# Logits in three rounded products, one key block among the first chunks, and a last half in two quarters

## The chip, the cores and the metric

The kernel runs on one core of a Trainium2 chip. The metric is the device time of one execution in microseconds (us). The engines are TensorE (PE; its weight loads are PEld), VectorE (DVE), ScalarE (ACT), GpSimd (POOL) and SyncE (SP, which only issues transfers here).

## The reference

A trunk of two layers on 512 tokens of 1024 values. Layer A mixes by gated linear attention (six heads) and attention into 256 memory tokens; layer B by stick-breaking attention (twelve heads of 64) and memory attention. After each mixer come an output projection, a residual and a layer norm, and then PEER, a feed-forward layer of retrieved experts, with its own residual and layer norm.

```python
def gla_layer_mixer(x, mem, w_in, w_gate2, b_gate, head_g, w_mem_kv, w_out):
    proj = x @ w_in
    q, k, v, r, glr, qm = jnp.split(proj, A_IN_SPLITS, axis=-1)
    log_g = jax.nn.log_sigmoid((glr @ w_gate2 + b_gate).astype(jnp.float32)) / GLA_TAU
...
def stick_breaking(q, k, v):
    B, H, T, d = q.shape
    scale = d ** -0.5
    outs = []
    for i in range(T // SB_BLOCK):
        t0, t1 = i * SB_BLOCK, (i + 1) * SB_BLOCK
        z = jnp.einsum('bhtd,bhsd->bhts', q[:, :, t0:t1], k[:, :, :t1]).astype(jnp.float32) * scale
...
        log_A = jax.nn.log_sigmoid(z) + lax.cumsum(log_not, axis=3, reverse=True) - log_not
        A = jnp.where(mask, jnp.exp(log_A), 0.0).astype(v.dtype)
        outs.append(jnp.einsum('bhts,bhsd->bhtd', A, v[:, :, :t1]))
...
        h = layer_norm(DEEPNORM_ALPHA * h + mix, ln_g[layer, 0], ln_b[layer, 0])
        ffn = peer(h, peer_w_q[layer], peer_subkeys[layer], peer_u[layer], peer_v[layer])
        h = layer_norm(DEEPNORM_ALPHA * h + ffn, ln_g[layer, 1], ln_b[layer, 1])
```

## The kernel before, in words

Nearly all products are made of three: an operand is split into a rounded high part (fp32r, by ACT) and the rounded rest (by DVE), and high x high, high x low and low x high add up in PSUM. `stat_mm` does this for one block of 128 output rows over the eight chunks of the 1024 inner values, lines L117 to L119 for each chunk, 512 tokens at a time. `split` (L97 on ACT, L98 on DVE) makes the two parts. Several stretches are under a manual schedule: there the engines named run in the order in which the code is written.

*Start of mixer A.* `values_gates` multiplies all eight chunks of x (its transpose, loaded by `load_xT`, split at L470 and L471) with 272 weight columns (256 of values, 16 of gates; `load_vg`, split at L479 and L480), for four tiles of 128 tokens, three matmuls each (L498 to L500, tile `vga`). SP issues the loads in the order of the calls, and ACT and DVE do the splits in that order too. Then `stat_units` goes through eight blocks (`as` is the load, `ash` and `asl` its halves, `asp` the result in PSUM): blocks 0 to 2 the keys, 3 to 5 the queries, 6 and 7 the memory queries. `ev_stat` copies each to SBUF with ACT. Between them `gate_logits` puts its transposes (`pgl`, L513) and the later gate work.

*Mixer B.* The twelve heads go in six pairs. For a pair, one `bsp` block holds the keys and one the queries, 64 rows for each head; `ev_stat` (L744) copies them to SBUF as `kq`, queries times 0.125. `logits` (L764, tile `pz`) multiplies them by blocks of 128 queries against all keys up to that block: query block 3 (512 columns), blocks 2 and 0 (384 and 128), and block 1 (256), in plain fp32. The first head has array rows 0 to 63, the second 64 to 127, each with its own PSUM buffer. DVE clips at L767 (`zs`), ACT takes exponent and logarithm (L771, L777), DVE scans and subtracts (L782, L783), ACT exponentiates (L787). `turn` transposes the weights of an earlier pair (`pt`, L796) and copies them out with DVE (L800) or ACT (L802); `attend` multiplies them with the values (`pav`, L810). One period of the loop (j = 1 to 5) makes the logits of pair j, the weights of pair j - 1 turned, and the next pair's blocks; the last makes the values instead (`bva`). PE, DVE and ACT run in the written order there.

*End.* The last tile of the last PEER takes its six tail matrices for the first half of 512 columns, then for the second half (L1789 to L1791, `acc`, 18 matmuls each). `layer_norm` then makes y = alpha x + acc (L993), the statistics (L995), their aggregate (L998) and the scaled result (L1002 to L1010), which goes out by DMA (L1675).

Of the kernel before, what the change touches and what calls it, by code (L numbers as in the profile page):

```python
# [10 lines left out]
F32 = mybir.dt.float32  # L11
# [63 lines left out]
def psum(E, name="ps", tag="ps"):  # L75
    p, tags = E.ps
    return p.tile([P, 512], F32, tag=tag, name=name, bufs=tags[tag])
# [48 lines left out]
def stat_units(E, src, blks, evac, xhi=None, xlo=None, n=T, name="sp", tag="ps"):  # L126

    for b in blks:
        hi, lo = split(E, load_raw(E, src[b], name), name)
        ps = psum(E, name=f"{name}p", tag=tag)  # L130
        stat_mm(E, ps[:, :n], hi, lo, xhi, xlo)
        evac(b, ps[:, :n])
        yield
# [279 lines left out]
def mixer_a(E, a):  # L413
# [4 lines left out]
    with tc.tile_pool(name="acat", bufs=1, reuse_waits="tile") as ap:  # L418
# [11 lines left out]
        with psum_pool(E, acc=4, ps=4), tc.tile_pool(name="mixwk", bufs=2, reuse_waits="tile") as wk, \  # L430
# [52 lines left out]
            def values_gates():  # L483

                acc = [psum(E, name="vga", tag="acc") for _ in range(NT)]
                ws = load_vg(0, 1)
                load_xT(0, 1)
                load_xT(1, 1)
                ws += load_vg(1, 2)
                load_xT(2, 2)  # L490
                load_xT(4, 2)
                ws += load_vg(3, 3)
                load_xT(6, 2)
                ws += load_vg(6, 2)
                for c, h, l in ws:
                    for t in range(NT):
                        xh, xl = E.xhi[:, c, t * P:(t + 1) * P], E.xlo[:, c, t * P:(t + 1) * P]
                        nc.tensor.matmul(acc[t][:, :VG], xh, h, start=(c == 0), stop=False)  # L498
                        nc.tensor.matmul(acc[t][:, :VG], xl, h, start=False, stop=False)
                        nc.tensor.matmul(acc[t][:, :VG], xh, l, start=False, stop=(c == NC - 1))  # L500
                for t in range(NT):
                    twice = gl[:, t, :64].rearrange("p (a b) -> p a b", a=2)[:, :, :16]
                    nc.scalar.activation(twice, acc[t][:, None, 256:VG].to_broadcast([P, 2, 16]), AF.Copy)
                    nc.vector.tensor_sub(gl[:, t, 64:80], acc[t][:, 256:VG], gl[:, t, :16].bitcast(F32))
                for t in range(NT):
                    nc.vector.tensor_copy(v[:, t, 512:], acc[t][:, :256])
# [119 lines left out]

            with tc.manual_schedule(engines={mybir.EngineType.PE}):
                values_gates()
                st = stat_units(E, wst, range(8), ev_stat, name="as")
                logits = gate_logits()  # L630
                for _ in st:
                    next(logits, None)
# [84 lines left out]
def mixer_b(E, wst, wnat, wo, lng, lnb):  # L717

    nc, tc = E.nc, E.tc
    with tc.tile_pool(name="bcat", bufs=1, reuse_waits="tile") as cp:  # L720
# [10 lines left out]
        with tc.tile_pool(name="mbx", bufs=1, reuse_waits="tile") as mp, tc.tile_pool(name="mbwk", bufs=2, reuse_waits="tile") as wk:  # L731
# [3 lines left out]

            kq = {}

            def ev_stat(b, ps):
                if b >= 12:
                    dst = qm[:, b - 12]  # L740
                else:
                    dst = wk.tile([P, T], F32, tag=("kT", "qT")[b % 2], name="kq", bufs=1)
                    kq[b] = dst
                act.append(nc.scalar.activation(dst, ps, AF.Copy, scale=0.125 if b < 12 and b % 2 else 1.0))  # L744

            tiles, act = {}, []

            def logits(g, tags=("z",)):

                two = (g, g + 1)  # L750
                for h in two:
                    zs = wk.tile([P, 1280], F32, tag="zs", name="zs") if g % 4 else new_zs("zs", 1280)
                    tiles[h] = zs, wk.tile([P, 1280], F32, tag="ez", name="ez", bufs=4)
                kT, qT = kq[g], kq[g + 1]
                for n, qs in enumerate(((3,), (2, 0), (1,))):
                    if n:
                        yield
                    pz = [psum(E, name="pz", tag=tags[n % len(tags)]) for _ in two]
                    w, o = sum(i + 1 for i in qs) * P, QO[qs[0]]
                    for i in qs:  # L760
                        c = QO[i] - o
                        for k in range(2):
                            rows = slice(64 * k, 64 * k + 64)
                            nc.tensor.matmul(pz[k][:, c:c + (i + 1) * P], qT[rows, i * P:(i + 1) * P], kT[rows, :(i + 1) * P], start=True, stop=True)  # L764
                    m = (3 - qs[0]) * P
                    for k, h in enumerate(two):
                        nc.vector.tensor_tensor(tiles[h][0][:, o:o + w], pz[k][:, :w], lim[:, m:m + w], op=ALU.min)  # L767
# [90 lines left out]
            with psum_pool(E, ps=2, z=4, c=2), tc.manual_schedule(engines={eng.PE, eng.DVE, eng.Activation}):  # L858
# [11 lines left out]
                def stat(b, ps=None):  # L870

                    ps = ps or psum(E, name="bsp")
                    hi, lo = parts.pop(b)
                    for c in range(NC):
                        stat_mm(E, ps, hi, lo, cs=(c,))
                        yield
                    ev_stat(b, ps)
                    yield

                vacc = []  # L880

                def values(u):

# [24 lines left out]
                for j in range(1, 6):  # L908
# [1 line left out]
                    last = j == 5  # L910
                    zz = logits(h)
                    turn(g, 0, "v")
                    turn(g, 1, "v")
                    next(zz)
                    next(zz)
                    turn(g, 2, "v")
# [14 lines left out]
                    steps(fill)  # L931
                    remain(h)
                    remain(h + 1)
                    weights(h)
                    if not last:
                        fill = stat(h + 3)
# [2 lines left out]
                        prep(*((wst, h + 4) if j < 4 else (wnat, 4)))()  # L939
                        weights(h + 1)  # L940
                        steps(fill)
                        low.append(prep(*((wst, h + 5) if j < 4 else (wnat, 5))))
                    else:
                        late = []
# [36 lines left out]
def layer_norm(E, lp, t, halves, gam, bet, hooks=()):  # L981
# [2 lines left out]
    nc = E.nc  # L984
    y = lp.tile([P, D], F32, tag="lny", name="lny", bufs=1)
    wd = min(h.shape[-1] for h in halves)
    st = E.lnp.tile([P, 2, 6], F32, tag="lnst", name="lnst", bufs=2)
    mv = E.lnp.tile([P, 2], F32, tag="lnmv", name="lnmv", bufs=2)
    sm = E.lnp.tile([P, 4], F32, tag="lnsm", name="lnsm", bufs=2)
    c = 0  # L990
# [67 lines left out]
LEAD = 3  # L1058
TAIL = 6
G3 = 96  # L1060
WOI = 3
RB = 4
SEG = [(0, 1, 0, 16, 16), (1, 1, 16, 8, 8), (2, 1, 24, 8, 5), (3, 1, 32, 8, 4), (4, 1, 40, 4, 3), (5, 3, 44, 4, 2), (8, 8, 56, 1, 1)]
# [2 lines left out]
def peer(E, mixer, wq, sk, ut, vt, un, lng, lnb, out_dram=None, follow=()):  # L1066
# [10 lines left out]
    with ExitStack() as pp:  # L1077
# [659 lines left out]
        with written:  # L1737
# [39 lines left out]
            for t in range(ND):  # L1777
                sl = slice(t * P, (t + 1) * P)
                parts = acc[t]
                if t < ND - 1:  # L1780
                    for k, (whi, wlo, hi, lo) in enumerate(tail):
                        mov_mm(E, parts, whi[:, sl], wlo[:, sl], hi, lo, False, k == TAIL - 1)
                else:
                    c = 0
                    for a in parts:
                        hs = slice(c, c + a.shape[-1])
                        c = hs.stop
                        for k, (whi, wlo, hi, lo) in enumerate(tail):
                            nc.tensor.matmul(a, whi[:, sl], hi[:, hs], start=False, stop=False)  # L1789
                            nc.tensor.matmul(a, whi[:, sl], lo[:, hs], start=False, stop=False)  # L1790
                            nc.tensor.matmul(a, wlo[:, sl], hi[:, hs], start=False, stop=k == TAIL - 1)  # L1791
                if last:
                    finish(t + 1, parts)
                elif t < ND - 1:
                    if t == 0:
                        E.low.pop(0)()
                    finish(t + 1, parts, (lambda: x_to_T(E, t), lambda: E.low.pop(0)()))
                else:
                    finish(t + 1, parts)
# [87 lines left out]
```

## Time and profile before

| | us |
|---|---|
| median of 3 runs | 2839.48 |
| lowest, highest | 2837.48, 2840.02 |
| profiled execution, its own time | 2838.77 |
| its span in the trace | 2837.0 |
| value gates and key block 0 of mixer A | 5.18 to 26.23 |
| one period of mixer B (second of the loop) | 1513.71 to 1532.27 |
| start of the last matmul | 2828.20 |

The span runs from the first to the last record of the trace; the execution's own time has 1.8 us around it. In the rows of the trace stand a start, a length, the engine, the line, the operation, out<-in by the program's names, the shape and, in brackets, the idle time before it with the one that ended it.

### The profile page before, as it was taken

Reading aid. Unit: us, or ns where it says so; the run is one execution under the profiler, and the core shown is the slowest. Engines: PE = TensorE matmul, PEld = TensorE weight load, DVE = VectorE, ACT = ScalarE, POOL = GpSimd, SP = SyncE. Lnnn points to the kernel's source line nnn. Section 1 sums busy time; section 2 is a strip of 40 time slices with the busy share of each in tenths; the row PEclk is TensorE's granted clock in tenths of the full one; section 3 lists DMA queues with packets and bytes.
Section 4 is the critical chain, followed back from the end, with each engine's and each line's share of the span. In section 5 each row is a group of like instructions: output and inputs, shape, how many; then the busy total and the mean of one; then the engine's idle time right before and its main releaser. Section 6 shows DMA issues by size and latency. Waiting matters only on the chain.

```text
span 2837.0 us, 44540 instructions
## 1 busy us (share of the span) xinstructions
PE 2820.4 (99%) x16141; PEld 2509.1 (88%) x16141; DVE 2407.4 (85%) x4917; ACT 1444.6 (51%) x2724; POOL 783.6 (28%) x585
## 2 busy tenths in 40 slices
PE   9999999999999999999999999999999999999998
PEld 8888999999999888888887889999999998888887
DVE  5567999999886888888968879999998878888888
ACT  6342447767774333334446424476677743334333
POOL 0100243333342233245100002433334433333330
PEclk9999999999999999999999999999999999999999
DMA  6332589999999999999721325999999999999994
GB/s 203 101 109 74 179 308 331 334 328 337 352 365 344 341 371 372 366 358 378 238 68 52 112 84 199 317 320 334 335 339 340 379 334 351 372 372 371 370 371 170
DMA packets 311150, 806.99 MB, mean 284 GB/s; under 512 B 32177, under 2 KB 124561, under 8 KB 304529
## 3 DMA queue, kind: packets, MB, share of 16 engines
q1 hardware_dynamic: 195936, 414.93, 42.2%
q0 software_dynamic: 78336, 285.25, 27.7%
q10 hardware_dynamic: 36656, 103.97, 9.5%
q8 instruction: 126, 2.06, 0.3%
q14 instruction: 96, 0.78, 0.1%
HBM read 708.32 MB, written 94.68 MB: 283 GB/s over the span
## 4 chain that ended last, share of the span: by engine, by line
PE 91%; DVE 7%; DMA 1%; issue 1%; ACT 0%; DVEq 0%; ACTq 0%
PE ph L117 11%; PE acc L289 11%; PE acc L291 11%; PE acc L293 11%; PE ph L119 11%; PE ph L118 11%; PE pg L1525 2%; PE pg L1526 1%; DVE ul L98 1%; PE pq L117 1%; PE pq L118 1%; PE pq L119 1%; PE bsp L117 1%; PE bsp L119 1%; PE bsp L118 1%; PE oacc L289 1%
## 5 line engine op out<-in xcount | busy, mean ns | idle before, releaser
L117 PE MATMUL ph<-xhi,uh 128*128 128x368 f32 x2048 | 686.9, 335 | 0.0
L119 PE MATMUL ph<-xhi,ul 128*128 128x368 f32 x2048 | 674.5, 329 | 1.1 <-DVE ul L98 0.8
L118 PE MATMUL ph<-xlo,uh 128*128 128x368 f32 x2048 | 673.5, 329 | 0.0
L1116 POOL DMA_INDIRECT gr<-in_un,gidx x256 | 394.0, 1539 | 802.4 <-DVE gr L1169 588.6
L97 ACT ACTIVATE vh<-vr 128x1024 fp32r<-128x1024 f32 x248 | 262.8, 1060 | 502.2 <-PE acc L293 418.8
L1116 POOL DMA_INDIRECT gr<-in_vt,gidx x256 | 314.2, 1227 | 652.5 <-DVE va L1188 565.4
L289 PE MATMUL acc<-vh,whi 128*128 128x512 f32 x1480 | 455.9, 389 | 0.6 <-ACT whi L1732 0.6
L291 PE MATMUL acc<-vl,whi 128*128 128x512 f32 x1480 | 455.7, 389 | 0.0
L293 PE MATMUL acc<-vh,wlo 128*128 128x512 f32 x1480 | 455.6, 389 | 0.0
L98 DVE TENSOR_TENSOR vl<-vr,vh 128x1024 fp32r<-128x1024 f32 x248 | 303.6, 1224 | 151.1 <-ACT vh L97 150.1
L97 ACT ACTIVATE uh<-ur 128x1024 fp32r<-128x1024 f32 x288 | 304.2, 1056 | 191.9 <-PE ph L118 147.5
L98 DVE TENSOR_TENSOR ul<-ur,uh 128x1024 fp32r<-128x1024 f32 x288 | 351.3, 1220 | 43.6 <-ACT uh L97 42.0
L119 PEld LDWEIGHTS ph<-xhi,ul 128*128 128x128 f32 x2048 | 384.7, 188 | 3.5 <-DVE ul L98 3.5
L118 PEld LDWEIGHTS ph<-xlo,uh 128*128 128x128 f32 x2048 | 385.4, 188 | 0.0
L117 PEld LDWEIGHTS ph<-xhi,uh 128*128 128x128 f32 x2048 | 385.1, 188 | 0.1
L289 PEld LDWEIGHTS acc<-vh,whi 128*128 128x128 f32 x1480 | 277.6, 188 | 58.8 <-ACT whi L1732 1.5
L291 PEld LDWEIGHTS acc<-vl,whi 128*128 128x128 f32 x1480 | 277.7, 188 | 58.0 <-DVE vl L98 0.4
L293 PEld LDWEIGHTS acc<-vh,wlo 128*128 128x128 f32 x1480 | 277.7, 188 | 57.8 <-DVE wlo L1733 0.3
L1169 DVE SCALAR_TENSOR_TENSOR gr<-gr,xnat 128x1024 f32<-128x1024 f32 x256 | 310.0, 1217 | 19.5 <-DMA gr<-in_un,gidx 19.2
L1188 DVE SCALAR_TENSOR_TENSOR va<-gr,gw,va 128x1024 f32<-128x1024 f32 x254 | 325.0, 1280 | 1.3 <-DMA gr<-in_vt,gidx 0.4
L1506 ACT ACTIVATE obl<-ob,rat 128x128 f16<-128x128 f16 x736 | 234.2, 392 | 31.3 <-ACT gt L1529 16.3
L1732 ACT ACTIVATE whi<-w 128x384 fp32r<-128x384 f32 x256 | 131.3, 513 | 96.8 <-DVE w L1721 92.5
(379 smaller groups left out, 4202.5 us busy)
## 6 DMA issues: line engine op xcount, KB each, us to landing
ur<-in_ut SPq DMA_DIRECT2D x256, 512.0 KB
vr<-in_vt SPq DMA_DIRECT2D x256, 512.0 KB
Gd<-gt ACTq DMA_DIRECT2D x48, 1024.0 KB
Ad<-act ACTq DMA_DIRECT2D x112, 368.0 KB
al<-Ad SPq DMA_DIRECT2D x112, 368.0 KB
gl<-Gd SPq DMA_DIRECT2D x26, 1536.0 KB
ur<-in_wq SPq DMA_DIRECT2D x32, 512.0 KB
bs<-in_b_st SPq DMA_DIRECT2D x14, 512.0 KB
```

What stands on the lines that cost most here:

```text
L97: nc.scalar.activation(hi, raw, AF.Copy)
L98: sub = lambda: eng.tensor_sub(lo, raw, hi.bitcast(F32))
L117: nc.tensor.matmul(ps, h, xhi[:, c, sl], start=(c == 0), stop=False)
L118: nc.tensor.matmul(ps, h, xlo[:, c, sl], start=False, stop=False)
L119: nc.tensor.matmul(ps, l, xhi[:, c, sl], start=False, stop=(c == NC - 1))
L289: nc.tensor.matmul(acc[hf], lh, hi[:, hf * 512:(hf + 1) * 512], start=first, stop=False)
L291: nc.tensor.matmul(acc[hf], lh, lo[:, hf * 512:(hf + 1) * 512], start=False, stop=False)
L293: nc.tensor.matmul(acc[hf], ll, hi[:, hf * 512:(hf + 1) * 512], start=False, stop=last)
L1116: nc.gpsimd.indirect_dma_start(out=gr, out_offset=None, in_=tab, in_offset=bass.IndirectOffsetOnAxis(ap=idx[:, k:k + 1], axis=0))
L1169: nc.vector.scalar_tensor_tensor(gr, gr, 1.0, xr, op0=ALU.mult, op1=ALU.mult, accum_out=dst[:, k:k + 1])
L1188: nc.vector.scalar_tensor_tensor(va, gr, gw[:, k:k + 1], va, op0=ALU.mult, op1=ALU.add)
L1506: nc.scalar.activation(obl[:, q], ob[:, q, 0], AF.Copy, scale=rat[:, n0 + q:n0 + q + 1])
```

## The change

Four edits. First, `values_gates` begins with six fp32 matmuls on the identity into an unused PSUM buffer (`idle`), loads key block 0 after the second load of weights, and lets that block's eight chunks follow the value gates one chunk behind; `stat_units` then has blocks 1 to 7. The load of weights 3 to 5 goes ahead of the x chunks 4 and 5. Second, in mixer B keys and queries are kept as a rounded high part (`kqh`, ACT) and a rounded rest (`kql`, a new DVE instruction that reads PSUM), and each logit product is three fp32r matmuls in place of one fp32 matmul, the two heads in turn; in the loop the rests are put off to two places (`rests`). Third, the copy of `turn(g, 1)` goes from DVE to ACT. Fourth, the last half of the last tile is done as two quarters of 256 columns, the first without a stop of its own, and that tile's statistics are taken by 256 columns.

```diff
             def values_gates():
 
                 acc = [psum(E, name="vga", tag="acc") for _ in range(NT)]
+                idle, pa = psum(E, name="idle"), psum(E, name="asp")
+                for _ in range(WARM):
+                    nc.tensor.matmul(idle[:, :P], E.ident, E.ident, start=True, stop=True)
+                place = mp.tile([P, 2, D], F32R, tag="mr", name="as0")
                 ws = load_vg(0, 1)
                 load_xT(0, 1)
                 load_xT(1, 1)
                 ws += load_vg(1, 2)
+                a0 = split(E, load_raw(E, wst[0], "as"), "as", lambda name: place[:, "hl".index(name[-1])])
                 load_xT(2, 2)
+                ws += load_vg(3, 3)
                 load_xT(4, 2)
-                ws += load_vg(3, 3)
                 load_xT(6, 2)
                 ws += load_vg(6, 2)
...
                         nc.tensor.matmul(acc[t][:, :VG], xh, l, start=False, stop=(c == NC - 1))
+                    if c:
+                        stat_mm(E, pa, *a0, cs=(c - 1,))
+                stat_mm(E, pa, *a0, cs=(NC - 1,))
+                ev_stat(0, pa)
...
-                st = stat_units(E, wst, range(8), ev_stat, name="as")
+                st = stat_units(E, wst, range(1, 8), ev_stat, name="as")
...
-            def ev_stat(b, ps):
+            def ev_stat(b, ps, later=None):
                 if b >= 12:
                     dst = qm[:, b - 12]
                 else:
-                    dst = wk.tile([P, T], F32, tag=("kT", "qT")[b % 2], name="kq", bufs=1)
-                    kq[b] = dst
-                act.append(nc.scalar.activation(dst, ps, AF.Copy, scale=0.125 if b < 12 and b % 2 else 1.0))
+                    tag, scale = (("kT", 1.0), ("qT", 0.125))[b % 2]
+                    dst = wk.tile([P, T], F32R, tag=tag, name="kqh", bufs=1)
+                    low = wk.tile([P, T], F32R, tag=tag + "l", name="kql", bufs=1)
+                    kq[b] = dst, low
+                    act.append(nc.scalar.activation(dst, ps, AF.Copy, scale=scale))
+                    rest = lambda: nc.vector.scalar_tensor_tensor(low, ps, scale, dst.bitcast(F32), op0=ALU.mult, op1=ALU.subtract)
+                    if later is None:
+                        rest()
+                    else:
+                        later.append(rest)
+                    return
+                act.append(nc.scalar.activation(dst, ps, AF.Copy))
...
-                        for k in range(2):
-                            rows = slice(64 * k, 64 * k + 64)
-                            nc.tensor.matmul(pz[k][:, c:c + (i + 1) * P], qT[rows, i * P:(i + 1) * P], kT[rows, :(i + 1) * P], start=True, stop=True)
+                        for m, (q_, k_) in enumerate(((0, 0), (0, 1), (1, 0))):
+                            for k in range(2):
+                                rows = slice(64 * k, 64 * k + 64)
+                                nc.tensor.matmul(pz[k][:, c:c + (i + 1) * P], qT[q_][rows, i * P:(i + 1) * P], kT[k_][rows, :(i + 1) * P],
+                                                 start=m == 0, stop=m == 2)
...
-                    turn(g, 1, "v")
+                    turn(g, 1, "a")
...
                     remain(h + 1)
+                    while rests:
+                        rests.pop()()
                     weights(h)
...
                         steps(fill)
+                        while rests:
+                            rests.pop()()
...
-    st = E.lnp.tile([P, 2, 6], F32, tag="lnst", name="lnst", bufs=2)
+    st = E.lnp.tile([P, 4, 6], F32, tag="lnst", name="lnst", bufs=2)
...
+WARM = 6
...
+                    if last:
+                        parts = [acc[t][0], acc[t][1][:, :256], acc[t][1][:, 256:]]
                     c = 0
-                    for a in parts:
+                    for n, a in enumerate(parts):
...
-                            nc.tensor.matmul(a, wlo[:, sl], hi[:, hs], start=False, stop=k == TAIL - 1)
+                            nc.tensor.matmul(a, wlo[:, sl], hi[:, hs], start=False, stop=k == TAIL - 1 and (n != 1 or not last))
```

DVE at the start of mixer A, before: after the weights of chunks 1 and 2 (`vgl` of 544 columns) come the two x pairs (`xlo` of 1024) and then the weights of chunks 3 to 5.

```order
4 L480 TENSOR_TENSOR vgl<-vg,vgh 128x544 [waits DMAHW6_49,Activation_49]
5 L516 TENSOR_TENSOR w_115<-w2r,w_115 32x384 [waits DMAHW0_49,Activation_49]
6 L471 TENSOR_TENSOR xlo<-xnat,xhi 128x1024 [waits DMAHW7_49,Activation_49]
7 L471 TENSOR_TENSOR xlo<-xnat,xhi 128x1024 [waits DMAHW0_49,Activation_49]
8 L454 CAST msk<-mf 128x128 [waits Pool_49]
9 L480 TENSOR_TENSOR vgl<-vg,vgh 128x816 [waits DMAHW1_49,Activation_49]
10 L471 TENSOR_TENSOR xlo<-xnat,xhi 128x1024 [waits DMAHW2_49,Activation_49]
```

The same place now; `as_148` is block 0's tile.

```order
4 L480 TENSOR_TENSOR vgl<-vg,vgh 128x544 [waits DMAHW6_49,Activation_49]
5 L525 TENSOR_TENSOR w_115<-w2r,w_115 32x384 [waits DMAHW0_49,Activation_49]
6 L98 TENSOR_TENSOR as_148<-as,as_148 128x1024 [waits DMAHW7_49,Activation_49]
7 L471 TENSOR_TENSOR xlo<-xnat,xhi 128x1024 [waits DMAHW0_49,Activation_49]
8 L454 CAST msk<-mf 128x128 [waits Pool_49]
9 L480 TENSOR_TENSOR vgl<-vg,vgh 128x816 [waits DMAHW1_49,Activation_49]
10 L471 TENSOR_TENSOR xlo<-xnat,xhi 128x1024 [waits DMAHW2_49,Activation_49]
11 L471 TENSOR_TENSOR xlo<-xnat,xhi 128x1024 [waits DMAHW3_49,Activation_49]
```

Block 0's low half stands where the first x pair stood; that pair stands where the second was, and the second comes after the weights of chunks 3 to 5.

DVE in a period of mixer B, from the second scan to the clipped logits, before:

```order
1944 L782 SCALAR_TENSOR_TENSOR ez<-go,ez 128x1280 [waits Activation_49]
1945 L783 TENSOR_TENSOR zs<-zs,ez 128x1280 [waits DVE_49]
1946 L192 TENSOR_TENSOR cat_15895<-pav,cat_15895 128x512 [waits Activation_49]
1947 L868 TENSOR_TENSOR bsl<-bs,bsh 128x1024 [waits DMAHW4_49,Activation_49]
1948 L800 COPY ez<-pt 128x512 [waits PE_49] x2
```

and now:

```order
1952 L802 SCALAR_TENSOR_TENSOR ez<-go,ez 128x1280 [waits Activation_49]
1953 L803 TENSOR_TENSOR zs<-zs,ez 128x1280 [waits DVE_49]
1954 L756 SCALAR_TENSOR_TENSOR kql<-bsp,kqh 128x512 [waits Activation_49]
1955 L192 TENSOR_TENSOR cat_15983<-pav,cat_15983 128x512 [waits Activation_49]
1956 L888 TENSOR_TENSOR bsl<-bs,bsh 128x1024 [waits DMAHW4_49,Activation_49]
1957 L756 SCALAR_TENSOR_TENSOR kql<-bsp,kqh 128x512 [waits Activation_49]
1958 L820 COPY ez<-pt 128x512 [waits PE_49]
1959 L787 TENSOR_TENSOR zs<-pz,lim 128x512 [waits PE_49] x4
```

The keys' rest (first `kql`) stands behind the subtraction, the queries' rest behind the split of the next block, and one copy of `pt` is gone from DVE.

DVE at the end of the program, the last tile's norm, now:

```order
3691 L1017 SCALAR_TENSOR_TENSOR lny<-xnat,acc_0_24938 128x512 [waits DVE_49,PE_49]
3692 L1019 BN_STATS lnst<-lny 128x6 [waits DVE_49]
3693 L1019 BN_STATS lnst<-lny 128x6
3694 L1017 SCALAR_TENSOR_TENSOR lny<-xnat,acc_1_24939 128x256 [waits PE_49]
3695 L1019 BN_STATS lnst<-lny 128x6 [waits DVE_49]
3696 L1017 SCALAR_TENSOR_TENSOR lny<-xnat,acc_1_24939 128x256
3697 L1019 BN_STATS lnst<-lny 128x6 [waits DVE_49]
3698 L1022 BN_AGGR lnmv<-lnst 128x2 [waits DVE_49]
```

Where one y and one statistic of 512 columns stood for the second half, there are two of each of 256; the first of these y's waits for PE, the second for nothing more.

More of the change, by code (lines that the diff above doesn't have):

```diff
@@ L876, in stat @@
                         yield
-                    ev_stat(b, ps)
+                    ev_stat(b, ps, rests)
                     yield
-                vacc = []
+                vacc, rests = [], []
                 def values(u):
```

## The prediction

> **What bounds the kernel now.** I read the page first, for the engine that carries the chain.
>
> ```profile
> span 2837.0 us, 44540 instructions
> PE 2820.4 (99%) x16141; PEld 2509.1 (88%) x16141; DVE 2407.4 (85%) x4917; ACT 1444.6 (51%) x2724; POOL 783.6 (28%) x585
> PE 91%; DVE 7%; DMA 1%; issue 1%; ACT 0%; DVEq 0%; ACTq 0%
> ```
>
> PE is busy for 99% of the span and carries 91% of the chain; DVE has 7%. A saving on PE therefore reaches the end, unless something else is late at that place. The next view is what PE waits for.
>
> ```profile
> PE vga L498 <- ACT xhi L470: 5.2, 1, 5.2
> PE ph L119 <- DVE ul L98: 0.8, 2, 0.4
> PE pz L764 <- DVE zs L767: 0.4, 1, 0.4
> PE vga L500 <- DVE vgl L480: 0.2, 1, 0.2
> ```
>
> The columns are total, times and longest. Only the first 5.2 us, before any data are split, are a large wait. No edit can win more than small pieces, in three places that I then read in the timeline: the start of mixer A, the periods of mixer B, and the last microseconds.
>
> **Start of mixer A.** PE, ACT and DVE from 5 to 26 us (start, length, engine, line):
>
> ```profile
> 5.18 0.59 PE L498 MATMUL vga<-vgh,xhi 128*128 128x272 f32 x1 [5.18 <-ACT xhi L470]
> 10.39 0.43 PE L500 MATMUL vga<-vgl,xhi 128*128 128x272 f32 x1
> 10.62 0.43 PE L498 MATMUL vga<-vgh,xhi 128*128 128x272 f32 x1
> 12.87 0.29 PE L499 MATMUL vga<-vgh,xlo 128*128 128x272 f32 x1
> 13.35 0.39 PE L500 MATMUL vga<-vgl,xhi 128*128 128x272 f32 x1 [0.19 <-DVE vgl L480]
> 20.64 0.29 PE L500 MATMUL vga<-vgl,xhi 128*128 128x272 f32 x1
> 20.76 0.40 PE L117 MATMUL asp<-xhi,ash 128*128 128x512 f32 x1
> 26.23 0.60 PE L513 MATMUL pgl<-ident,gl 128*96 128x128 f32 x4
> 8.65 1.06 ACT L470 ACTIVATE xhi<-xnat 128x1024 fp32r<-128x1024 f32 x1 [0.18 <-DMA xnat<-in_xT]
> 9.92 1.06 ACT L470 ACTIVATE xhi<-xnat 128x1024 fp32r<-128x1024 f32 x1 [0.22 <-DMA xnat<-in_xT]
> 9.74 2.50 DVE L471 TENSOR_TENSOR xlo<-xnat,xhi 128x1024 fp32r<-128x1024 f32 x2 [0.34 <-ACT xhi L470]
> 12.29 1.00 DVE L480 TENSOR_TENSOR vgl<-vg,vgh 128x816 fp32r<-128x816 f32 x1
> ```
>
> The 272-column matmuls start 0.23 us apart at 10.5 us and 0.12 ahead of the next one at 20.6: PE runs at half its later rate until about 11 us. Block 0 of the keys, 24 matmuls of 512 columns, takes 20.76 to 26.23, 0.227 each. So value gates and block 0 together end at 26.23.
>
> The change puts block 0's load between the pair of first weights and x chunks 2 and 3, and so its two splits take the places of that x pair: ACT at 8.65, DVE from 9.74 for 1.25 (half of 2.50). The x pair then takes the next places: ACT 9.92 to 10.98, DVE until about 12.2. PE meanwhile has chunks 0 and 1 (until about 11.1, as now) and one chunk of block 0, which fits into the gap. Then it waits for the low half of chunk 2, until 12.25. From there six chunks of gates (12 x 0.127 = 1.52 each) and seven of block 0 (3 x 0.227 = 0.68) are left: 12.25 + 9.1 + 4.8 = 26.15, less one matmul done ahead: about 26.0. The weights of chunks 3 to 5, ready at 13.3, are needed near 14.4, so the stall at 13.35 goes. **Term: -0.2 us.**
>
> The six idle matmuls run before 5.18, in time that is lost anyway. If they bring the full rate earlier, PE only comes earlier to the same wait at 12.25. All that could be won here is half a rate from 5.18 to 11 (2.9 us) and the stall (0.35), 3.2 us in all. The loss is bounded by one more place in the DVE line (1.25 us). Bounds: -3.2 to +1.3.
>
> The Trainium skill, page "TensorE: Matmul & The Clock Gate", Part 1, says that TensorE starts at half its clock and gets the full one after about 3.4 us of sustained activity, so a warm-up ahead of the data should pay. The trace agrees with the half rate, which lasts 5.8 us here. By the rule alone the start would gain up to the 2.9 us named above; by the rows the data decide, and the gain is 0.2.
>
> **Mixer B.** One period, from one group of heads to the next:
>
> ```profile
> 1512.94 0.60 ACT L744 ACTIVATE kq<-bsp 128x512 f32<-128x512 f32 x1 [0.69 <-PE bsp L119]
> 1513.71 2.00 PE L764 MATMUL pz<-kq 64*128 64x512 f32 x12
> 1515.63 0.87 PE L796 MATMUL pt<-ident,zs 128*128 128x128 f32 x6
> 1516.44 0.70 PE L764 MATMUL pz<-kq 64*128 64x256 f32 x4
> 1517.07 0.50 PE L117 MATMUL bsp<-xhi,bsh 128*128 128x512 f32 x1
> 1513.38 1.29 DVE L800 COPY ez<-pt 128x512 f32<-128x512 f32 x2 [0.71 <-PE pt L796]
> 1514.87 2.48 DVE L767 TENSOR_TENSOR zs<-pz,lim 128x512 f32<-128x512 f32 x4 [0.20 <-PE pz L764]
> 1516.60 0.60 ACT L802 ACTIVATE ez<-pt 128x512 f32<-128x512 f32 x1 [2.12 <-PE pt L796]
> 1517.60 0.75 DVE L767 TENSOR_TENSOR zs<-pz,lim 128x256 f32<-128x256 f32 x2
> 1529.18 0.69 DVE L192 TENSOR_TENSOR cat<-pav,cat 128x512 fp32r<-128x512 f32 x1
> 1531.94 1.29 DVE L800 COPY ez<-pt 128x512 f32<-128x512 f32 x2 [0.94 <-PE pt L796]
> 1513.71:1532.27 18.56, 18.56 (x101) 13.43 (x100) 16.17 (x17) 12.34 (x15) 0.00 (x0) 1.00 0.19 60
> 1513.71 0.70 PE L764 MATMUL pz<-kq 64*128 64x512 f32 x2
> ```
>
> The logits take PE 1.92 us (1513.71 to 1515.63) and 0.63 (1516.44 to 1517.07). The trace has two records for each fp32 matmul, which makes 12 of the six. The last row, a narrow window, shows the heads' two matmuls busy for 0.70 together, as long as the hardware takes for one: the two row groups run at the same time. Each head thus passes 2 x 1024 columns in about 1.7 us, and some 0.2 goes on the turn to the next kind.
>
> The rounded form goes over the columns three times, not twice, at 0.227 for 512. For 256 columns the trace has
>
> ```profile
> 1573.34 0.28 PE L894 MATMUL bva<-bsl,xhi 128*128 128x256 f32 x1
> 1573.46 0.28 PE L895 MATMUL bva<-bsh,xlo 128*128 128x256 f32 x1
> ```
>
> 0.12. On that line 384 columns are about 0.17 and 128 about 0.07. If the heads still run together: 3 x (0.227 + 0.17 + 0.07) + 0.2 = 1.60, and 3 x 0.12 + 0.2 = 0.56. That saves 0.39 of 2.55. Against it stands a new wait: the third product needs the query's low half. The high half is there at 1513.54, the DVE instruction takes 0.69 (L192's size), so 1514.23; PE, 0.45 after 1513.71, is at it by 1514.16. With the signal I take 0.1. Net **-0.29 in each of four periods; -1.2 us.** The first group (other order on DVE, no such slack) and the fifth I take at nothing: after the fifth comes a stretch in which DVE's scans and ACT's weights are the chain, and an earlier PE only waits longer.
>
> DVE is the cover. It is busy for 16.17 of 18.56; it gains two low halves (1.38) and loses a copy (0.65) to ACT, which has 2.12 idle just there: 16.9 of some 18.3. Its idle 0.94 ahead of the copies nearly goes. The copy (g,1) on ACT follows the split of 1.05 and ends near 1515.1, before PE wants its buffer. Where DVE no longer fits, PE's period is DVE's, and the gain goes. Bounds for all six groups: -0.5 each (128 columns at nothing, no wait) to +0.3 each (three loads of weights at 0.1 for 128 columns, the wait at 0.3), that is -3 to +2.
>
> **The tail.**
>
> ```profile
> 2828.20 0.39 PE L1791 MATMUL acc<-vh,wlo 128*128 128x512 f32 x1
> 2826.79 0.69 DVE L993 SCALAR_TENSOR_TENSOR lny<-xnat,acc 128x512 f32<-128x512 f32 x1
> 2827.51 0.70 DVE L995 BATCH_NORM_STATS2 lnst<-lny 128x6 f32<-128x512 f32 x1
> 2828.63 0.69 DVE L993 SCALAR_TENSOR_TENSOR lny<-xnat,acc 128x512 f32<-128x512 f32 x1 [0.42 <-PE acc L1791]
> 2829.35 0.69 DVE L995 BATCH_NORM_STATS2 lnst<-lny 128x6 f32<-128x512 f32 x1
> 2830.08 0.21 DVE L998 BATCH_NORM_AGGREGATE lnmv<-lnst 128x2 f32<-128x12 f32 x1
> ```
>
> After the last matmul DVE takes 0.72 for y, 0.73 for the statistics, then aggregates at 2830.08. The 18 matmuls of the second half become 36: 36 x 0.12 - 18 x 0.227 = +0.23. The first quarter has no stop of its own, and its y waits for PE only once, while the second quarter's y waits for nothing more; I read this as a wait for the last matmul of all, so nothing starts early. Then four operations of 256 columns stand in line where two of 512 stood. Two independent ones of L767 take 0.75, 0.34 from start to start; one that waits for the one ahead I put at 0.45, its 0.41 and the 0.03 seen between 512-column ones: 0.45 + 0.34 + 0.45 + 0.47 = 1.7 against 1.45. **Term: +0.23 + 0.27 = +0.5 us.** Bounds +0.2 (operations at half a 512's price) to +0.7. If the first quarter did start early, its two operations would hide under the second's 2.16 us of matmuls, and 0.23 - 0.55 = -0.3 would be left.
>
> **Sum.** -0.2 - 1.2 + 0.5 = -0.9 us. The profiled execution took 2838.77 (span 2837.0 and 1.8 around it), so 2837.9 on its own scale; it lies 0.7 under the median of 2839.48, so **2838.6**.
>
> **Rivals.** (a) *Rounded heads in the two row groups run one after the other.* Then the three passes of both heads cost 6 x 0.467 + 0.2 = 3.0 and 6 x 0.12 + 0.2 = 0.92, 1.37 more than now, in six groups: +8.2, and +0.3 from the other two terms: 2848, slower. It decides as soon as the second head starts more than 0.2 after the first. Against it: fp32 heads do run together (0.70 for two), for it: no rounded row group is in the trace. The same Clock Gate page, Part 3, holds that matmuls in different row groups run concurrently and names no type as an exception; no run here shows it for the rounded one. (b) *PE's rate, not the data, sets the start.* Then a full rate from the first matmul on wins the 2.9 us and the stall there, -3.2 instead of -0.2: 2835.6. For it: PE waits only once for a split before 26 us now; against it: the line of splits on DVE, without a gap from 9.74 to 13.3, gets one more ahead of what PE needs. This is where the clock page's rule would lead. (c) *DVE becomes the bound of mixer B*, one late split per period costing PE 0.4: +2 instead of -1.2, 2842. (d) *The first quarter starts early:* 0.8 less, 2837.8.
>
> **How the numbers follow.** My sum or near it (2836.5 to 2840.5) 0.62; (a) 0.08; (b) 0.07; (c) 0.12; (d) 0.08; all parts at their good ends at once, -3.2 - 3 + 0.2 = -6, 0.03. A measurement of this kernel tells about 0.2% (5.7 us) from no change; only (a) and the last case lie beyond it. So faster 0.03, same 0.89, slower 0.08. The range leaves out (a) and the last case, takes in the others, and has the spread of the runs (2.5 us) at its ends: 2834.5 to 2843.
>
> **What would show it.** The first 512-column start of block 0 near 11.1, one wait for xlo near 12, the transposes of the gates (pgl) at 26.0; with 23 instead, the start was PE's. In mixer B two heads' pz in 0.4 together for 512 columns; the period 18.3; a wait of pz for kql of 0.1. DVE's idle time ahead of the copies near zero and not a wait of PE. At the end y of 256 columns after the last matmul, the aggregate 2.0 after the last matmul's start against 1.9 now. Heads one after the other, or a period over 18.6, would make the prediction wrong.

## The result, and the profile after

The changed kernel takes 2867.96 us (median of 5 runs, 2867.63 to 2867.98), the kernel before 2839.48 (median of 5, 2837.48 to 2841.71): a ratio of 1.0101, 95% interval 1.009 to 1.0113. It is 1% slower. I had forecast 2838.6 and no change that can be measured.

The page of the changed kernel, first span, busy time and chain, then the groups of the value products in both PEERs (busy us, mean ns of one):

```profile
span 2865.8 us, 44710 instructions
PE 2852.2 (100%) x16219; PEld 2512.6 (88%) x16219; DVE 2413.6 (84%) x4927; ACT 1445.4 (50%) x2729; POOL 760.9 (27%) x585
PE 90%; DVE 9%; issue 0%; DMA 0%; ACT 0%; DVEq 0%; ACTq 0%
...
L289 PE MATMUL acc<-vh,whi 128*128 128x512 f32 x1480 | 464.1, 394 | 0.0
L291 PE MATMUL acc<-vl,whi 128*128 128x512 f32 x1480 | 464.1, 394 | 0.0
L293 PE MATMUL acc<-vh,wlo 128*128 128x512 f32 x1480 | 464.1, 394 | 0.0
```

The same three groups before:

```profile
L289 PE MATMUL acc<-vh,whi 128*128 128x512 f32 x1480 | 455.9, 389 | 0.6 <-ACT whi L1732 0.6
L291 PE MATMUL acc<-vl,whi 128*128 128x512 f32 x1480 | 455.7, 389 | 0.0
L293 PE MATMUL acc<-vh,wlo 128*128 128x512 f32 x1480 | 455.6, 389 | 0.0
```

PE is as dense as before, with more busy time, and the time is in lines that the change does not touch: each value product of the PEERs is longer, 394 ns against 389. These matmuls overlap, so the length of a record is not their price. The price is read from how many of them start in a fixed stretch. One of 400 us, inside the value stage of the first PEER, holds nothing but such products on PE (before, 24 of the tail products below are among them) (columns: stretch, its length, then for PE, PEld, DVE, ACT and POOL busy time and number; clock, DMA share, GB/s). Before:

```profile
1000.00:1400.00 400.00, 399.72 (x1764) 330.50 (x1763) 340.43 (x416) 161.60 (x301) 136.67 (x100) 1.00 0.99 357
```

After:

```profile
1000.00:1400.00 400.00, 400.00 (x1716) 320.59 (x1715) 332.59 (x399) 152.22 (x286) 112.64 (x102) 1.00 0.98 352
```

400 / 1764 is 226.8 ns, 400 / 1716 is 233.1, at the full granted clock in both and with hardly a wait (0.28 us before, none after): 6.3 ns more for each. The two value stages have 3 x 1464 such products ahead of their tails, 4,392: 27.7 us. That is nearly the whole difference of 28.5.

The tail matrices of the same stage (`vtail`) use the same `whi` and `wlo`, the same lines and the same PSUM tiles. Their rows in the changed kernel (shortest, median and longest ns, first and last start):

```profile
L291 PE MATMUL acc<-vtail,whi x32: 389/389/395, 1408.5 to 2845.2; 128*128 128x512 f32 x32
L293 PE MATMUL acc<-vtail,wlo x32: 389/389/393, 1409.0 to 2845.6; 128*128 128x512 f32 x32
```

They kept 389, and their median from start to start is 227. Four of the six tail matrices are in `vtail`; the last two, again named `vh` and `vl`, lie in another pool's buffers, and in the last tile of the first PEER they start 226 to 227 apart too. What differs between slow and fast products is only where the moving tile lies in SBUF. The addresses that I read in the two built programs (bytes within a partition; the traces do not carry them, so what rests on them is tested by moving the tiles below):

```
               before     after      after, modulo 256
whi (first)    170432     170496     0
vh (its three) 87744 91840 95936     192  (the same before and after)
vtail          112576     112640     0
```

Before, all three are 192 modulo 256. The statistics tile `lnst`, [P, 2, 6] made [P, 4, 6], lies in a pool that is opened ahead of all stages; its two buffers took 64 bytes each and take 96. Everything allocated behind it moved by 64 bytes, the buffers `vh` and `vl` ahead of it did not.

### The profile page after: what moved, and what is told of

Same layout as the page of the kernel before. It is cut to its first block, busy times and chain, and to the rows that moved or that the text cites. A ratio compares the mean times of both kernels' runs of the same rounds, so it can differ in the third digit from the quotient of the medians.

```text
span 2865.8 us, 44710 instructions
## 1 busy us (share of the span) xinstructions
PE 2852.2 (100%) x16219; PEld 2512.6 (88%) x16219; DVE 2413.6 (84%) x4927; ACT 1445.4 (50%) x2729; POOL 760.9 (27%) x585
## 4 chain that ended last, share of the span: by engine, by line
PE 90%; DVE 9%; issue 0%; DMA 0%; ACT 0%; DVEq 0%; ACTq 0%
PE acc L289 12%; PE acc L293 12%; PE acc L291 12%; PE ph L117 11%; PE ph L119 11%; PE ph L118 11%; DVE ul L98 2%; PE pg L1550 2%; PE pg L1551 1%; DVE gr L1194 1%; PE bsp L117 1%; PE oacc L293 1%; PE oacc L289 1%; PE oacc L291 1%; PE bsp L118 1%; PE bsp L119 1%
## 5 line engine op out<-in xcount | busy, mean ns | idle before, releaser
L1141 POOL DMA_INDIRECT gr<-in_vt,gidx x256 | 288.1, 1125 | 703.0 <-DVE va L1213 602.5
L289 PE MATMUL acc<-vh,whi 128*128 128x512 f32 x1480 | 464.1, 394 | 0.0
L291 PE MATMUL acc<-vl,whi 128*128 128x512 f32 x1480 | 464.1, 394 | 0.0
L293 PE MATMUL acc<-vh,wlo 128*128 128x512 f32 x1480 | 464.1, 394 | 0.0
L1554 ACT ACTIVATE gt<-pg 128x512 f32<-128x512 f32 x184 | 109.4, 594 | 91.0 <-PE pg L1551 62.6
```

Of the source, the lines that this page charges most:

```text
L289: nc.tensor.matmul(acc[hf], lh, hi[:, hf * 512:(hf + 1) * 512], start=first, stop=False)
L291: nc.tensor.matmul(acc[hf], lh, lo[:, hf * 512:(hf + 1) * 512], start=False, stop=False)
L293: nc.tensor.matmul(acc[hf], ll, hi[:, hf * 512:(hf + 1) * 512], start=False, stop=last)
L1141: nc.gpsimd.indirect_dma_start(out=gr, out_offset=None, in_=tab, in_offset=bass.IndirectOffsetOnAxis(ap=idx[:, k:k + 1], axis=0))
```

## The experiments

The theory: the 64 bytes between `whi` and `vh` cost the 28 us. The rival: the work of the change does it, by queues, clock or transfers.

**The change with its addresses put back, and the address shift alone.** Two kernels and a bench.

```diff
-    st = E.lnp.tile([P, 4, 6], F32, tag="lnst", name="lnst", bufs=2)
+    if wd == 256:
+        st = lp.tile([P, 4, 6], F32, tag="lnst4", name="lnst4", bufs=1)
+    else:
+        st = E.lnp.tile([P, 2, 6], F32, tag="lnst", name="lnst", bufs=2)
```

> The changed kernel, with the statistics tile of the last norm in another pool, so that every SBUF address after it is that of the kernel before. Theory P (the larger statistics tile moved whi and wlo by 64 bytes against vh and vl, and each of the some 4,460 acc matmuls of both PEERs takes 6.4 ns longer for that): acc back at 389 ns a piece, 227 ns from start to start, the time 28 to 29 us under the changed kernel, about 2839. Rival Q (the time comes from the change's own work, what it does to queues, clock or transfers): acc stays at 394 ns, about 2868.

Measured: 2838.15 us (11 runs, 2836.78 to 2839.45) beside 2837.85 for the kernel before, ratio 1.0001, interval 0.9992 to 1.001. The stretch of 400 us has

```profile
1000.00:1400.00 400.00, 400.00 (x1766) 331.20 (x1766) 344.28 (x417) 161.35 (x303) 112.70 (x100) 1.00 0.99 357
```

226.5 ns. All four edits are in this kernel; they cost nothing that can be measured.

```diff
-    st = E.lnp.tile([P, 2, 6], F32, tag="lnst", name="lnst", bufs=2)
+    st = E.lnp.tile([P, 4, 6], F32, tag="lnst", name="lnst", bufs=2)
```

> The kernel before, with nothing but its statistics tile made four groups large, two of them unused. P: acc at 394 ns, 233 from start to start, 2867 to 2869 us. Q: no difference, 2839 to 2840.

Measured: 2867.94 us, ratio 1.0106 (1.0091 to 1.0122), with

```profile
1000.00:1400.00 400.00, 400.00 (x1716) 320.56 (x1715) 332.81 (x399) 152.18 (x286) 112.86 (x102) 1.00 0.98 352
```

The kernel before, with 32 unused bytes more in each of the two buffers of a tile that these products never read, is as slow as the changed one. The rival falls.

**Which places are dear.** The bench is a kernel of its own, rows of 32 matmuls from one pair of places each:

```python
def unit(n, s, m, name):
    a = pp.tile([P, 512], F32, tag="u", name=name, bufs=4)
    for r in range(REP):
        w = s // 4 + (r % 4) * P
        nc.tensor.matmul(a[:, :n], W[:, w:w + P], M[:, m // 4:m // 4 + n], start=(r == 0), stop=(r == REP - 1))
```

> Nothing of the computation but rows of 32 matmuls on rounded data, for 512, 384, 368, 256 and 128 moving columns, each with the stationary and the moving tile at other places (s and m in the name are the bytes past a multiple of 128). P with the difference of the two places modulo 128 as what counts: 227 ns at 512 columns for differences 0 and 128 and 256, 233 for 64, the same for s64m0 as for s0m64; at 256 columns 120 for 0 and 117 for 64, as the trace of before has for pq and mkp. P with the absolute place: s64m64 unlike s0m0. Q: one spacing for all places of a size.

Each row below is the stretch from the first to the last start of one unit of 512 columns, 31 steps (columns: stretch, length, PE busy and number, clock, DMA share, GB/s). In their order: s0m64, s0m128, s0m192, s64m0, s32m32, s256m0.

```profile
30.02:37.12 7.10, 7.10 (x32) 1.00 0.01 2
44.83:52.06 7.23, 7.23 (x32) 1.00 0.00 0
59.78:67.02 7.24, 7.24 (x33) 1.00 0.01 2
81.99:89.23 7.24, 7.24 (x33) 1.00 0.00 0
111.56:118.59 7.03, 7.03 (x32) 1.00 0.00 0
140.87:147.90 7.03, 7.03 (x32) 1.00 0.00 0
```

Divided by 31: 229.0, 233.2, 233.5, 233.5, 226.8, 226.8. At 512 columns the difference of the two places decides: s64m0 is as slow as s0m192, the same difference modulo 256, and s32m32 as fast as s256m0. But 128 is slow, so my modulo 128 was wrong; 256 apart is fast. The six rows of equal places at the full rate lie between 226.6 and 228.0, and the same place twice (s0m256) differs by 0.5. DMA is silent here, and no other engine reads the tiles, so transfers are not needed for it. The other widths gave (ns from start to start, worked out in the same way):

| columns | m - s = 0 (s32m32) | 128 | 192 |
|---|---|---|---|
| 368 | 167.0 | 173.1 | 168.9 |
| 256 | 119.6 | 118.8 | 114.0 |

At 256 columns another place is best, and there the difference alone does not decide: s64m0 has the difference of s0m192 and gave 117.8, not 114.0. At 384 columns equal places gave 173.3 to 174.2 and the others 173.2 to 176.7, which is no order by place; at 128 columns every place gave 111.6 or 111.7, but for 110.0 in the first row.

> Nothing of the computation but rows of 32 matmuls as in place_bench: the stationary tile at 0, the moving tile at every 8 bytes up to 248, for 512, 368 and 256 columns. Modulo 256 as a window: 227 ns at 512 columns for 0 and for some bytes around it, 229 around 64, 233 for the rest, with the edges at whole 8 or 16 columns. If only exact equality counts: 227 at 0 alone.

At 512 columns all steps of 8 bytes from 8 to 248 gave 228.8 to 239.8. The row at 0 came first, still at the slow rate of the start, so equality is read from the first bench. The nearest neighbours of zero, 8 and 248:

```profile
22.01:29.25 7.24, 7.24 (x32) 1.00 0.00 0
245.98:253.12 7.14, 7.14 (x33) 1.00 0.00 0
```

7.24 / 31 = 233.5 and 7.14 / 31 = 230.3. There is no window around zero. Equality modulo 256 is the cheapest place; the next is 64 bytes, 228.8 here and 229.2 and 229.5 in the first bench, only some 1 ns above the dearest equal row. The 368 and 256 columns of this bench gave 164.5 to 173.4 and 114.0 to 121.5, in no order that I can name.

**The same in the kernel.** `w`, the tile ahead of `whi` in its pool, is made wider and the rest not used, so that `whi` and `wlo` move and `vh` and `vl` do not:

```diff
-            w = wv.tile([P, TD], F32, tag="w", name="w")
+            w = wv.tile([P, TD + 16], F32, tag="w", name="w")[:, :TD]
```

(TD + 24 and TD + 32 for 192 and 256 bytes.)

> The kernel before, with the tile w of the value stage 64 bytes wider in each of its two buffers and not used there, so that whi and wlo alone stand 128 bytes further on. If places count by their difference modulo 256 (the bench has 233.5 ns at 128): 233 from start to start for all 4,608 matmuls, +30 us, 2868 to 2870. If modulo 128: no difference, 2838.

> The same with 96 bytes, whi and wlo 192 further on, so that the moving tile stands 64 past the stationary one modulo 256. Modulo 256 as the bench has it (228.9 ns for s0m64 and s64m128): 4,608 x 2.2 ns, +10 us, 2847 to 2850. Modulo 128: 2868.

> The kernel before with w 128 bytes wider in each buffer: whi and wlo 256 bytes further on, the same place as before modulo 256. If the pair of places counts modulo 256: 227 from start to start, 2837 to 2840, no difference from before. If any move of whi and wlo against the rest costs (another tile, a longer way in memory): 232 or more, 2860 or more.

Measured: 2863.73 us at 128 (ratio 1.0086, 1.0069 to 1.0103); 2867.74 at 192 (1.0101, 1.0084 to 1.0117), with four executions at 2858.5 and 2867.7 to 2868.1; 2840.89 at 256 (1.0007, 0.9998 to 1.0017). Rows of 128, of 192 in the first and the second PEER, and of 256:

```profile
1000.00:1400.00 400.00, 400.00 (x1723) 324.25 (x1723) 334.22 (x402) 153.61 (x289) 112.41 (x101) 1.00 0.98 351
```
```profile
1000.00:1400.00 400.00, 400.00 (x1749) 328.23 (x1748) 340.37 (x411) 157.85 (x298) 113.22 (x101) 1.00 0.99 356
2400.00:2800.00 400.00, 400.00 (x1716) 324.01 (x1715) 332.42 (x393) 153.04 (x289) 117.57 (x106) 1.00 1.01 360
```
```profile
1000.00:1400.00 400.00, 400.00 (x1766) 331.24 (x1765) 344.16 (x417) 161.04 (x303) 110.92 (x100) 1.00 0.99 358
```

232.2 ns at 128, 226.5 at 256: modulo 256 holds in the kernel too, and modulo 128 does not. The time at 128 is 4 us under the forecast's 2868, since 232.2 is under its 233. At 192 the bench's 229 (first row, 228.7) and 233 (second, 233.1) stand in one execution. That is the one of 2858.5; the other three of the same program took 9.2 to 9.6 us longer, and the 2,304 products of one PEER at 4.4 ns more each would be 10.1, so in those both PEERs were probably slow (an estimate from these rows; the three have no trace). My forecast of +10 us thus missed: at an unequal place the size is not fixed by the place alone.

**The four edits one by one.** With the addresses settled, the small terms can be read in the traces. The stages of the PEERs differ by 1 to 3 us from execution to execution without any edit, so I read each term inside its own stage.

> Only the first edit (idle matmuls, key block 0 among the first chunks) on the kernel before; addresses after it unchanged. My sum: the last matmul of the eight blocks (asp) starts 0.2 to 0.4 us earlier than the 65.34 of before, because the low half of chunks 2 and 3 comes one place later and PE waits for it near 12. Rival (PE's rate sets the start): 3 us earlier, near 62.3.

One execution, 2838.38 us. PE around the wait, with the steps that show its rate:

```profile
10.23 0.43 PE L504 MATMUL vga<-vgh,xlo 128*128 128x272 f32 x1
10.46 0.43 PE L505 MATMUL vga<-vgl,xhi 128*128 128x272 f32 x1
10.91 0.30 PE L504 MATMUL vga<-vgh,xlo 128*128 128x272 f32 x1
11.05 0.29 PE L505 MATMUL vga<-vgl,xhi 128*128 128x272 f32 x1
11.17 0.40 PE L117 MATMUL asp<-xhi,as 128*128 128x512 f32 x1
12.19 0.40 PE L504 MATMUL vga<-vgh,xlo 128*128 128x272 f32 x1
```

Block 0 begins at 11.17 and the wait for the low half ends at 12.19, as worked out. The step goes from 0.23 to 0.14 at 10.9; before, it did so near 11.1. But the rise moves from execution to execution, so this one pair does not tell what the idle matmuls do. In the seven traces of the big kernel without them it comes between 8.7 (shift_256) and 11.2 (shift_128); in those with them at 10.9 here, 9.8 in the changed kernel, 9.1 in after_home and 9.9 in best2, and in best (below), with the same idle matmuls, the first product of the data is already at the full rate:

```profile
5.14 0.39 PE L503 MATMUL vga<-vgh,xhi 128*128 128x272 f32 x1 [0.62 <-ACT xhi L470]
6.11 0.29 PE L505 MATMUL vga<-vgl,xhi 128*128 128x272 f32 x1
6.23 0.28 PE L503 MATMUL vga<-vgh,xhi 128*128 128x272 f32 x1
12.40 0.40 PE L504 MATMUL vga<-vgh,xlo 128*128 128x272 f32 x1 [0.66 <-DVE xlo L471]
```

Whether the idle matmuls bring the rise forward is open. What an early full rate is worth is not: with it PE waits for the same low half, until 12.40, and the last asp of the eight blocks starts at 65.44, against 65.34 before. The data set the start, not PE's rate. That last asp starts at 65.21 here, 65.04 in after_home and 66.10 in best2; in p_logits_v and p_tail, which lack this edit, at 65.48 and 65.06. The term of -0.2 is within what executions differ.

The logits alone, with the copy of `turn(g, 1)` left on DVE:

> Only the rounded logits, with the copy of turn(g, 1) left on DVE. If DVE is the bound without that move: periods of mixer B at 18.6 us or more (before 18.56), PE waiting for kql or for a pt copy in each. If DVE has room even so: periods of 18.3, as in after_home. In either case the stretch ahead of the loop loses 0.5 to 0.6 us, since the keys' low half of the second pair stands ahead of the mpT copies for which PE waits before mo.

One execution, 2840.57 us. First `bsp`, first `pt` and first `bva` of mixer B; before, then after_home, then p_logits_v:

```profile
1420.60 0.28 PE L117 MATMUL bsp<-xhi,bsh 128*128 128x256 f32 x1
1493.96 0.33 PE L796 MATMUL pt<-ident,zs 128*128 128x128 f32 x1
1572.77 0.38 PE L893 MATMUL bva<-bsh,xhi 128*128 128x256 f32 x1
```
```profile
1419.59 0.28 PE L117 MATMUL bsp<-xhi,bsh 128*128 128x256 f32 x1
1493.40 0.33 PE L816 MATMUL pt<-ident,zs 128*128 128x128 f32 x1
1571.30 0.39 PE L913 MATMUL bva<-bsh,xhi 128*128 128x256 f32 x1
```
```profile
1419.65 0.28 PE L117 MATMUL bsp<-xhi,bsh 128*128 128x256 f32 x1
1493.53 0.33 PE L807 MATMUL pt<-ident,zs 128*128 128x128 f32 x1
1573.11 0.38 PE L904 MATMUL bva<-bsh,xhi 128*128 128x256 f32 x1
```

The loop takes 78.81 before, 77.90 with the copy on ACT, and 79.58 with it on DVE. So one copy of 0.65 in each of five periods is worth 1.7 us: with it DVE is the bound (in p_logits_v it is busy for all 4.75 us from 1513.25 to 1518.00), without it just not. Ahead of the loop both lose: 73.36, 73.81, 73.88. The place is `mo`; after_home has there

```profile
1461.62 0.68 DVE L756 SCALAR_TENSOR_TENSOR kql<-bsp,kqh 128x512 fp32r<-128x512 f32 x1
1462.22 1.28 DVE L383 COPY mpT<-mpt 128x512 f32<-128x512 f32 x2
1462.95 2.53 PE L393 MATMUL mo<-mpT,Vm 128*64 128x512 f32 x8
```

where the kernel before had

```profile
1462.77 1.28 DVE L383 COPY mpT<-mpt 128x512 f32<-128x512 f32 x2
1463.99 2.04 PE L393 MATMUL mo<-mpT,Vm 128*64 128x512 f32 x8
```

The new instruction stands ahead of the copies, and `mo` stretches by 0.5. Two kernels tried to take that back. The first leaves out the quarters and puts the second pair's `kql` behind the copies:

```diff
-                one(2)
+                two = []
+                stat_proj(E, wst, range(2, 3), lambda b, ps: ev_stat(b, ps, two), name="bs")
...
                     f(1)
+                two.pop()()
```

> First, second and third edit, without the quarters, and with the second pair's kql behind the mpT copies. If the 0.5 to 0.6 us ahead of the loop come from that order: mo to the next msc back at 2.0 us, from the first bsp of mixer B to the first pt of the loop 73.2 us (before 73.36, after_home 73.81), the span about 1.4 us under that of before, 2835.5. If they come from something else: 73.8 again, 2836. A difference of this size lies within the timing's interval; the trace decides it.

Measured: 2838.14 us, ratio 1.0001 (0.9992 to 1.001). The loss stayed, 73.84 from the first `bsp` (1418.99) to the first `pt` (1492.83); only its place changed, since `mo` takes the PSUM buffer that `kql` still reads (it starts at 1462.93, after 0.65 of idle time that `kql` ends). The second keeps the order and gives one copy to ACT:

```diff
-                if mt == 0:
+                if mt == 0 and not (fine and j == 0 and hh == 1):
                     nc.vector.tensor_copy(pTs[hh][:, mt], ptp)
```

> First, second and third edit without the quarters; of the four mpT copies of the first memory unit in mixer B one goes from DVE to ACT. If DVE's queue (kql, two mpT copies) in front of mo is what costs the 0.48 us ahead of the loop: from the first bsp to the first pt of the loop 73.3 us or less, against 73.81 and 73.85. If it is the PSUM buffer that mo shares with bsp and nothing else: 73.8 again.

Measured: 73.22 (1420.19 to 1493.41). DVE's work ahead of `mo` was the cost, and with one copy gone the stretch is 0.14 shorter than before. One execution, 2839.59 us, beside 2838.88 for the kernel before: its gain of about 1 us in mixer B is not to be seen in the time (its last asp, 66.10, came 0.76 later than that of the trace before), so no version tried is measurably faster than the kernel before.

> Only the two quarters, with the statistics tile in the norm's own pool. My sum: the last matmul starts about 0.3 us later after the first acc matmul of the last half, and from its start to the end of the span 9.0 us instead of 8.8: +0.5. If the first quarter started early: y of 256 columns begins before the last matmul, -0.3.

One execution, 2840.39 us. The tail of after_home, and the same shape in p_tail:

```profile
2827.17 0.28 PE L1821 MATMUL acc<-vh,wlo 128*128 128x256 f32 x1
2827.49 0.42 DVE L1020 SCALAR_TENSOR_TENSOR lny<-xnat,acc 128x256 f32<-128x256 f32 x1 [0.60 <-PE acc L1821]
2828.29 0.40 DVE L1020 SCALAR_TENSOR_TENSOR lny<-xnat,acc 128x256 f32<-128x256 f32 x1
2829.19 0.26 DVE L1025 BATCH_NORM_AGGREGATE lnmv<-lnst 128x2 f32<-128x24 f32 x1
```

The first quarter's y waits for the last matmul of all, so rival (d) did not happen. From that matmul's start to the aggregate it is 2.02 (1.88 before), and to the end of the span 9.0 (8.8 before).

## Why the prediction was wrong

- **The step that failed** is the part on the tail. It priced the four quarter operations and the 36 matmuls, and gave the larger statistics tile no term at all. That tile's size was the whole result: 28.5 us, where the work of the tail costs half a microsecond. The deeper step is one that I did not write down: that the duration of a line which the change does not touch carries over from the trace of before. None of the rivals doubted it, so the range could not hold the time.
- **Rival (a)** did not happen. In after_home the products of the two heads go together, a pair of 512 columns every 0.23 (the step from the first row to the second), and the first group's logits take 1.60 (1438.69, its first product, to 1440.29), the number worked out for a group that waits for nothing:

```profile
1439.03 0.40 PE L783 MATMUL pz<-kql,kqh 64*128 64x512 f32 x2
1439.26 0.39 PE L783 MATMUL pz<-kqh,kql 64*128 64x512 f32 x2
...
1440.29 0.47 PE L355 MATMUL msc<-KmT,qm 64*128 64x256 f32 x2
```

- **Mixer B's term** was -1.2. The loop gave -0.91, the stretch ahead of it +0.45, the end of the stage +0.14 (19.26 to 19.40 from the first `bva` to the out projection): -0.32. In a period of the loop (the second, in after_home) the first group of logits takes 1.86 (1512.74 to 1514.60), not the 1.60 and 0.1 worked out. Its three pairs of 512 columns start at 1512.74, 1513.08 and 1513.35 and the next pair at 1513.69, the third behind the low half of the queries. The steps are 0.34, 0.27 and 0.34 where 0.23 was reckoned for each, 0.26 in all where 0.1 was reckoned for the wait; the period became 18.42, 0.14 less than 18.56 and not 0.29 less. I had taken the first group at nothing, with the order on DVE in view, but not the memory unit behind it, whose copies wait in the same queue. That DVE just fits, and only with the copy moved, was right.
- **The start**, -0.2, is too small to be told from what executions differ; that the data set it, and not PE's rate (rival (b)), was right. **The tail**, +0.5, came as worked out: +0.35 more between the starts of the last half's matmuls (35 x 0.12 against 17 x 0.2265), 0.14 to the aggregate and 0.05 in it. My mark for the start (`pgl` at 26.0) was a wrong one: `pgl` now follows block 1.
- After the addresses are put back, the sum of -0.9 stands against a measured ratio of 1.0001 (0.9992 to 1.001). That the four edits' own work gives no change that can be measured was right; the -0.9 is not confirmed by it. The terms that the traces show, -0.32 and +0.54, add up to +0.2, and the time cannot tell the two sums apart.

## What to carry to other kernels

A tile's size is part of a change: whatever is allocated behind it moves. When lines that an edit does not touch get slower by a constant per instruction at the same clock, with no wait, compare the addresses of their operands first; count starts in a fixed stretch, for records overlap, and their mean length showed 5 ns of the 6.3. Put a tile that only one place needs into that place's own pool.

## What the runs showed of the hardware

- A rounded (fp32r) matmul with 128 stationary and 512 moving columns, one after another, starts every 226.6 to 228.0 ns when the two SBUF operands have the same place modulo 256 bytes, and every 228.8 to 239.8 at all other places tried, in steps of 8 bytes (232.4 to 233.5 at 128 and 192, 228.8 to 229.5 at 64); at 256 columns the order is another (119.6 at equal places, 114.0 at s0m192). Why is open; no run here tests a mechanism. The Trainium skill, page "SBUF — State Buffer", section "Operand start alignment", asks only that an operand start at a multiple of its element size; all places here do, and the runs show that they are not alike in time.
- At an unequal place the price is not constant: 228.7 ns in the first PEER and 233.1 in the second of one execution of shift_192.
- The time at which PE reaches its full rate differs between executions: in those without idle matmuls 3.4 us (shift_256) to 6.0 us (shift_128) after the first product. The Trainium skill's page "TensorE: Matmul & The Clock Gate", Part 1, asks for some 3.4 us of sustained activity; no rise here came sooner after the first matmul than that (best, with idle matmuls from 1.59, was at the full rate by 5.14), and most came later.
